# A transformer-like layer in float32 on one core: the end of the last group of steps, rewritten

## The chip, the cores and the metric

The kernel runs on one core of a Trainium2 chip. The metric is device time in microseconds of one execution, as the median of several. The engines of the core are TensorE (PE; its weight loads are listed apart as PEld), VectorE (DVE), ScalarE (ACT), GpSimd (POOL) and SyncE (SP), which only issues transfers. Each has its own queue of instructions, worked off in order, and waits on semaphores of the others.

## The reference

One layer on x (256 tokens x 2048), with a mixer block, a convolutional MLP and a last RMSNorm. Only the end of it is touched here:

```python
def conv_ffn(x, g_norm, w_up, conv_k, conv_b, w_down):
    h = rms_norm(x, g_norm)
    up = h @ w_up
    ...
    gate, val = jnp.split(up, 2, axis=-1)
    return x + (jax.nn.silu(gate) * val) @ w_down
...
    return rms_norm(x, norm_final)
```

`w_down` is 5504 x 2048. `rms_norm` divides each row by the root of its mean square (plus 1e-6) and multiplies by the weight `g`, element by element.

## The kernel before

All products of activations and weights are in a float32 form split in two: each operand is a high part (`whi`, rounded by ScalarE, L267) and a low part (`wlo`, the rest, made by VectorE, L270), and a product is three matmuls (`three_products`, L398 to L400): high by high, low by high, high by low.

The weights come in one long list of pieces of 128 x 1024 through the SP queue into five buffers `wraw`. The main loop goes through the pieces in order: for piece i it issues loads, splits the pieces up to i + 4 (`prepare`), runs the tasks that were put down for i (`at(i, f)`, `run_tasks`), and then the piece's matmuls (`steps[key](i)`). Nothing is scheduled by a tool: the order in which this loop writes the instructions is the order on each engine.

The last group of pieces is `("down", 1, 1)`: 21 row tiles of `w_down` (21 x 128 rows) for output columns 1024 to 2047. `wide_step` (L457) keeps four sums in PSUM banks, one for each (b, c): b is the block of 128 tokens (also called t), c the half of the 1024 columns; in terms of the output, column quarter q = 2 + c. Some pairs of pieces are computed with seven products instead of eight; their extra sums are put together by `combine` (L488), which is three small functions `one`, `two`, `three` of VectorE and ScalarE instructions that add into the residual `x2`.

In this last group alone the last four pieces (`LAST = 4`) are held back and done block by block: for (0,0), (0,1), (1,0) and (1,1) in turn, 4 x 3 matmuls of 512 columns finish the bank, and `done` evaluates it at once. So the last 48 matmuls are four runs of twelve.

`done` leads to `finish(p, t, q)` (L1174) for these four banks. It adds the bank to `x2` (`add_down`, L1050, or L1186), squares it on ScalarE with a running sum into `ss[:, t, q]` (L1158, L1187), and at q = 3 makes the reciprocal root of the row (`root`, L1206 to L1214), scales the row's four quarters by it (`scaled`, L1216) and issues their transfers to DRAM. The final weight `g` is multiplied in ahead of the scaling: for q = 0 and 1 on VectorE in the group before, for q = 2 on GpSimd (L1179), for q = 3 on VectorE into a tile of its own (L1192). `root` is a square root on ScalarE, a reciprocal on VectorE, and one Newton step of three VectorE instructions (L1211 to L1213).

The rows of block t = 0 go out in parts of 1024, 512 and 512 columns, those of t = 1 in parts of 896 (columns 640 to 1535, ScalarE, in its own queue), 640 and 512 (VectorE, in SP's queue).

Of the kernel before, what the change touches and what calls it, by code (L numbers as in the profile page):

```python
# [8 lines left out]
F32 = mybir.dt.float32  # L9
# [147 lines left out]
def trunk_kernel(ctx, tc, x, weights, vectors, ln_g, ln_b, w_s_turned, b_s, rpb, norm_final, out):  # L157
# [299 lines left out]
    def wide_step(key, acts, sevens, rest, done, by_block=0, fresh=None):  # L457
# [30 lines left out]
        def combine(i):  # L488
# [34 lines left out]
                at(i + 2, two_fresh)  # L523
                return
            for n, f in enumerate((one, two, three)):
                at(i + 3 if by_block else i + 1 + n, f)

        def step(i):
            n = i - n0
# [10 lines left out]
            elif n - 1 in firsts:  # L540
                k = tiles[n - 1]
                ht, lt, _ = units[i - 1, "t"]
                hs, ls, _ = units[i - 1, "s"]
                S = sevens(k)
                product(5, S[0], (ht[:, c0], lt[:, c0]))
                product(7, S[2], (ht[:, c1], lt[:, c1]))
                unit_done((i - 1, "t"))
                product(6, S[1], (hs[:, c1], ls[:, c1]))
                product(4, acts(k + 1, 1), (hs[:, c0], ls[:, c0]))
                unit_done((i - 1, "s"))  # L550
                if n - 1 == firsts[-1]:
                    combine(i)
            elif n < size - by_block:
                h, l, _ = units[i]
                for (b, c), u in OUT.items():
                    cs = slice(c * 512, (c + 1) * 512)
                    product(u, acts(tiles[n], b), (h[:, cs], l[:, cs]))
                unit_done(i)
            elif n == size - 1:
                for (b, c), u in OUT.items():  # L560
                    for m in range(size - by_block, size):
                        h, l, _ = units[n0 + m]
                        cs = slice(c * 512, (c + 1) * 512)
                        product(u, acts(tiles[m], b), (h[:, cs], l[:, cs]))
                    done(p(u), b, c, i + 1)
                    free(p(u))
                for m in range(size - by_block, size):
                    unit_done(n0 + m)
            if n == size - 1 and not by_block:
# [603 lines left out]

    def finish(p, t, q):  # L1174
        x2, ss = rs["x2"], fin["ss"]
        if q == 2:
            add_down(p, t, 2)
            v = x2[:, t, 1024:1536]
            nc.gpsimd.tensor_mul(v, v, fin["g", 2])  # L1179
            if t == 0:  # L1180
                first_squares(0)
            else:
                scaled(0, 1024, 1536, nc.vector, nc.sync)
            return
        v = x2[:, t, 1536:]
        nc.vector.tensor_add(v, p, v)  # L1186
        nc.scalar.activation(junk, v, AF.Square, accum_out=ss[:, t, 3:4])  # L1187
# [4 lines left out]
        nc.vector.tensor_mul(y, v, fin["g", 3])  # L1192
# [12 lines left out]

    def root(t):  # L1206
        a, r, q, e, both = (const.tile([128, 1], F32, name=f"{n}3{t}") for n in "arqeb")
        nc.vector.tensor_scalar(a, fin["ss"][:, t, 3:4], 1.0 / D, fin["part", t], op0=OP.mult, op1=OP.add)
# [3 lines left out]
        nc.vector.tensor_scalar(e, e, -0.5, 1.5, op0=OP.mult, op1=OP.add)  # L1212
        nc.vector.tensor_mul(both, r, e)  # L1213
        fin["r", t] = both  # L1214

    def scaled(t, c0, c1, engine, queue):  # L1216
        v, r = rs["x2"][:, t, c0:c1], fin["r", t]
        u = fin["y", t] if c1 == D else v
        if engine is nc.scalar:
            nc.scalar.activation(v, u, AF.Copy, scale=r)  # L1220
        else:
            nc.vector.tensor_scalar(v, u, r, None, op0=OP.mult)
        queue.dma_start(out[0, t * 128:(t + 1) * 128, c0:c1], v)


# [70 lines left out]

    before = {}

    def open_attention():
        xin_st.close()  # L1300
        A, at_pool["st"] = pool("attn")
        at_pool["p"] = A
# [3 lines left out]
        at_pool["v"] = A.tile([128, NBLK, NAW], F32, name="vw")  # L1306
        bias_start(starts["u", 1] + 2, 0)

    before["u", 1] = open_attention

    def open_merge():
        G_st.close()
        mg["p"], mg["st"] = pool("merge", "right")

    before["qk", 0] = open_merge

    def close_attention():
        assert at_pool["done"] == HEADS // 2
# [14 lines left out]
    before["branch", 0, 1] = close_attention  # L1333
    rs["ss"] = const.tile([128, NT, 4], F32, name="ss_2")

    def open_x2():
        mg["st"].close()
        y_st.close()
        xp, xp_st = pool("x2", "right")
# [5 lines left out]
        ctx.push(f_st)  # L1345
        more_units(p)

    at(starts["out", 0] + 2, open_x2)

    def open_ff():  # L1350
        mg["m_st"].close()
        ff["a"], fa_st = pool("act")
        ctx.push(fa_st)

        def open_conv():
            ff["p"], conv_st = pool("conv", "right")
            ctx.push(conv_st)

        at(starts["up", 0] + 3, open_conv)

    before["up", 0] = open_ff
    fin["ss"] = const.tile([128, NT, 4], F32, name="ss_3")

    def load_fin():
# [55 lines left out]
```

## Time and profile before

| | us |
|---|---|
| median of 3 runs | 1310.52 (1310.21 to 1310.73) |
| the profiled execution's own time | 1310.8 |
| its span, first to last instruction | 1308.7 |
| PE busy in the span | 1296.1 |
| DVE, ACT, POOL busy | 1015.0, 746.4, 100.6 |
| DMA, mean over the span | 200 GB/s |
| granted TensorE clock | 0.997 of full speed |

The page of the profile lists busy times, groups of instructions by line, and the chain of work that ended last, followed back from the last instruction. Times in the timeline are microseconds from the span's start. A row of the timeline has start, duration, engine, line, operation and operands; in brackets is the idle time of the engine before it and what ended that. Tile names are cut to their stem: `x` is the residual `x2`, `h` a tile that holds a quarter of the final weight or, where L1192 writes it and L1222 reads it, its product with the fourth quarter of `x2`, `a`, `q`, `r`, `e`, `b` the one-column tiles of `root`.

### The profile page before, as it was taken

The page shows a single profiled execution, that of the slowest core. Times are in us where ns is not written, and L with a number is a line of the kernel's source. Part 1 is how long each engine was busy: PE and PEld are TensorE (multiplying, and loading weights), DVE is VectorE, ACT ScalarE, POOL GpSimd, SP SyncE. Part 2 cuts the span into 40 slices and gives each one's busy share as a digit, 9 for nine tenths or more (in the row PEclk, how much of TensorE's full clock was granted, in tenths as well). Part 3 has the DMA queues.
Part 4 walks back from the last instruction along what each step waited for, and adds up shares of the span by engine and source line. Part 5 has one row for each costly group of instructions (what it writes and reads, how often), then busy time and mean ns, then how long its engine had stood idle before and what let it go on. Part 6 is the DMA issues. An engine that isn't in the chain of part 4 may idle for free.

```text
span 1308.7 us, 18617 instructions
## 1 busy us (share of the span) xinstructions
PE 1296.1 (99%) x6754; PEld 1107.3 (85%) x6754; DVE 1015.0 (78%) x1484; ACT 746.4 (57%) x1103; POOL 100.6 (8%) x192
## 2 busy tenths in 40 slices
PE   9999999999999999999999999999999999999996
PEld 8888888888888888888888888888888888888885
DVE  6576667777588978887878787898958787869986
ACT  6755567576545555556655555564536555546553
POOL 0502065430000000000000000000000000000000
PEclk9999999999999999999999999999999999999998
DMA  9956675645647566665666656456655556646743
GB/s 347 318 177 199 206 223 185 201 162 178 192 156 246 173 203 237 224 207 179 192 194 185 200 180 207 162 184 229 210 183 192 192 193 194 192 131 225 250 152 129
DMA packets 73900, 261.42 MB, mean 200 GB/s; under 512 B 9552, under 2 KB 10704, under 8 KB 73296
## 3 DMA queue, kind: packets, MB, share of 16 engines
q1 hardware_dynamic: 69840, 252.46, 59.1%
q0 software_dynamic: 3680, 7.30, 2.1%
q8 instruction: 53, 0.87, 0.3%
q10 hardware_dynamic: 288, 0.47, 0.1%
q14 instruction: 39, 0.32, 0.1%
HBM read 256.00 MB, written 2.10 MB: 197 GB/s over the span
## 4 chain that ended last, share of the span: by engine, by line
PE 96%; DVE 1%; DMA 1%; ACT 1%; issue 0%; POOL 0%; ACTq 0%; POOLq 0%; DVEq 0%
PE bank L374 31%; PE bank L382 16%; PE bank L398 15%; PE bank L400 15%; PE bank L399 15%; PE bank L415 1%; PE bank L416 1%; PE bank L418 1%; DMA wraw<-in_weights_dram 1%; PE bank L878 1%; DVE wlo L270 0%; PE bank L930 0%; PE bank L609 0%; DVE x L1044 0%; PE bank L752 0%
## 5 line engine op out<-in xcount | busy, mean ns | idle before, releaser
L270 DVE TENSOR_TENSOR wlo<-wraw,whi 128x1024 fp32r<-128x1024 f32 (+1 forms) x476 | 569.3, 1214 | 143.4 <-ACT whi L267 132.4
L267 ACT ACTIVATE whi<-wraw 128x1024 fp32r<-128x1024 f32 (+1 forms) x476 | 487.9, 1046 | 221.5 <-PE bank L399 72.7
L374 PE MATMUL bank<-h,whi 128*128 128x512 f32 x1760 | 415.8, 391 | 0.0
L374 PEld LDWEIGHTS bank<-h,whi 128*128 128x128 f32 x1760 | 324.6, 188 | 64.4
L382 PEld LDWEIGHTS bank<-h,wlo 128*128 128x128 f32 x1760 | 215.9, 188 | 6.1
L382 PE MATMUL bank<-h,wlo 128*128 128x256 f32 x1760 | 218.7, 280 | 0.0
L398 PE MATMUL bank<-whi,h 128*128 128x512 f32 x284 | 111.9, 394 | 0.0
L400 PE MATMUL bank<-wlo,h 128*128 128x512 f32 x284 | 110.7, 390 | 0.0
L399 PE MATMUL bank<-whi,h 128*128 128x512 f32 x284 | 110.6, 389 | 0.0
L744 DVE TENSOR_TENSOR ta<-bank,tb 128x256 f32<-128x256 f32 x110 | 39.0, 416 | 76.6 <-ACT tb L742 76.6
L742 ACT ACTIVATE tb<-bank 128x256 f32<-128x256 f32 x110 | 36.2, 384 | 106.5 <-PE bank L374 101.9
L400 PE MATMUL bank<-wlo,a 128*128 128x512 f32 x248 | 96.6, 389 | 0.0
L398 PE MATMUL bank<-whi,a 128*128 128x512 f32 x248 | 96.5, 389 | 0.0
L399 PE MATMUL bank<-whi,a 128*128 128x512 f32 x248 | 96.5, 389 | 0.0
L1107 ACT ACTIVATE tc<-ta,vec 128x256 f32<-128x256 f32 x86 | 47.1, 595 | 84.3 <-DVE ta L1105 84.3
L398 PEld LDWEIGHTS bank<-whi,h 128*128 128x128 f32 x284 | 53.3, 188 | 11.3 <-DVE g L518 0.4
L400 PEld LDWEIGHTS bank<-wlo,h 128*128 128x128 f32 x284 | 53.3, 188 | 11.3
L399 PEld LDWEIGHTS bank<-whi,h 128*128 128x128 f32 x284 | 53.4, 188 | 10.6
L400 PEld LDWEIGHTS bank<-wlo,a 128*128 128x128 f32 x248 | 46.5, 188 | 10.1 <-DVE wlo L270 0.4
L398 PEld LDWEIGHTS bank<-whi,a 128*128 128x128 f32 x248 | 46.6, 188 | 9.7
L399 PEld LDWEIGHTS bank<-whi,a 128*128 128x128 f32 x248 | 46.5, 188 | 9.6
L1367 POOL DMA_DIRECT2D h<-in_norm_final_dram x4 | 2.2, 540 | 669.8 <-PE bank L382 669.1
(208 smaller groups left out, 1586.3 us busy)
## 6 DMA issues: line engine op xcount, KB each, us to landing
wraw<-in_weights_dram SPq DMA_DIRECT2D x446, 512.0 KB, 4.4
start<-in_weights_dram SPq DMA_DIRECT2D x13, 640.0 KB, 6.0
xs<-in_x_dram SPq DMA_DIRECT2D x2, 1024.0 KB, 8.2
vw<-va POOLq DMA_DIRECT2D x32, 64.0 KB, 6.0
x<-in_x_dram POOLq DMA_DIRECT2D x2, 1024.0 KB, 8.5
wraw<-in_weights_dram SPq DMA_DIRECT2D x8, 256.0 KB, 2.8
run<-in_rpb_dram POOLq DMA_DIRECT2D x64, 31.2 KB, 4.1
start<-in_weights_dram SPq DMA_DIRECT2D x3, 384.0 KB, 4.9
```

What stands on the lines that cost most here:

```text
L267: nc.scalar.activation(h, w, AF.Copy)
L270: nc.vector.tensor_sub(l, w, h.bitcast(F32))
L374: nc.tensor.matmul(p, h[:, c:c + 128], acts(2 * n + k), start=n == 0 and k == 0, stop=n == last and k == tiles - 1)
L382: nc.tensor.matmul(p[:, :T], l[:, c:c + 128], acts(2 * n + k)[:, 0, :], start=False, stop=False)
L398: nc.tensor.matmul(p, xh, wh, start=start, stop=False)
L399: nc.tensor.matmul(p, xl, wh, start=False, stop=False)
L400: nc.tensor.matmul(p, xh, wl, start=False, stop=stop)
L415: nc.tensor.matmul(p, xh, h[:, cs], start=n == 0, stop=False)
L416: nc.tensor.matmul(p, xl, h[:, cs], start=False, stop=False)
L742: nc.scalar.activation(t, p[:, T:], AF.Copy)
L744: nc.vector.tensor_add(a, p[:, :T], t)
L1107: nc.scalar.activation(v, u, AF.Identity, scale=ck[:, 1, ch:ch + 1], bias=ck[:, 3, ch:ch + 1])
```

## The change

Seven things, all in the last group:

- The bank (1,1) is finished in two halves. Twelve matmuls of 256 columns finish columns 0 to 255 of the bank; then the whole bank of 512 columns is added to `x2`, where columns 256 to 511 still lack the last four pieces. Twelve more matmuls of 256 columns put these four pieces into a fresh bank, and `last_quarter` adds it.
- The sums of squares of t = 1, q = 3 are taken in two instructions of 256 columns, the second into a tile `ss_q`.
- GpSimd does no multiplication any more. At t = 0, q = 2 the weight is multiplied on VectorE. For t = 0, q = 3 and for t = 1, q = 2 and 3, weight and scale are one instruction on VectorE (`scalar_tensor_tensor`: x times r times g).
- The Newton step works on -4 times the mean square, so that its last two instructions become one.
- `root` and the scaling of the first 1024 columns of t = 0 are moved from the evaluation of (0,1) to the start of that of (1,0), before its add.
- The rows of t = 1 go out in four parts of 512 columns, two scaled by ScalarE (one in SP's queue, one in ScalarE's), two by VectorE (in SP's queue).
- The function `one` of `combine` runs a piece earlier in this group (`i + 2` instead of `i + 3`).

Some inner functions are also renamed (`open_attention` to `firstattention` and the like), which changes no instruction.

```diff
             for n, f in enumerate((one, two, three)):
-                at(i + 3 if by_block else i + 1 + n, f)
+                at(i + (2, 3, 3)[n] if by_block else i + 1 + n, f)
...
             elif n == size - 1:
+                rows = range(size - by_block, size)
+
+                def products(q, b, c0, c1, first):
+                    for m in rows:
+                        h, l, _ = units[n0 + m]
+                        three_products(q, acts(tiles[m], b), (h[:, c0:c1], l[:, c0:c1]), first and m == rows[0],
+                                       m == rows[-1])
+
                 for (b, c), u in OUT.items():
-                    for m in range(size - by_block, size):
-                        h, l, _ = units[n0 + m]
-                        cs = slice(c * 512, (c + 1) * 512)
-                        product(u, acts(tiles[m], b), (h[:, cs], l[:, cs]))
+                    if (b, c) != (1, 1):
+                        products(p(u), b, c * 512, (c + 1) * 512, False)
+                        done(p(u), b, c, i + 1)
+                        free(p(u))
+                        continue
+                    products(p(u)[:, :256], b, 512, 768, False)
                     done(p(u), b, c, i + 1)
                     free(p(u))
+                    q = bank()
+                    products(q[:, :256], b, 768, 1024, True)
+                    last_quarter(q[:, :256])
+                    free(q)
...
     def finish(p, t, q):
         x2, ss = rs["x2"], fin["ss"]
-        if q == 2:
-            add_down(p, t, 2)
-            v = x2[:, t, 1024:1536]
-            nc.gpsimd.tensor_mul(v, v, fin["g", 2])
-            if t == 0:
-                first_squares(0)
-            else:
-                scaled(0, 1024, 1536, nc.vector, nc.sync)
+        v = x2[:, t, q * 512:(q + 1) * 512]
+        if (t, q) == (1, 2):
+            root(0, ss[:, 0, 3:4])
+            scaled(0, 0, 1024, nc.scalar, nc.sync)
+        if (t, q) == (1, 3):
+            add_rest(p, t, q)
+            nc.scalar.activation(junk[:, :256], v[:, :256], AF.Square, accum_out=ss[:, 1, 3:4])
             return
-        v = x2[:, t, 1536:]
+        add_down(p, t, q)
+        if (t, q) == (0, 3):
+            nc.vector.tensor_mul(x2[:, 0, 1024:1536], x2[:, 0, 1024:1536], fin["g", 2])
+            first_squares(0)
+        if (t, q) == (1, 2):
+            scaled(0, 1024, 1536, nc.vector, nc.sync)
+            scaled(0, 1536, 2048, nc.vector, nc.sync)
+
+    def last_quarter(p):
+        v, s = rs["x2"][:, 1, 1792:], const.tile([128, 1], F32, name="ss_q")
         nc.vector.tensor_add(v, p, v)
-        nc.scalar.activation(junk, v, AF.Square, accum_out=ss[:, t, 3:4])
-        if t == 1:
-            first_squares(1)
-            scaled(0, 1536, 2048, nc.vector, nc.sync)
-        y = fin["y", t] = hpool.tile([128, 512], F32, name=f"h{t}")
-        nc.vector.tensor_mul(y, v, fin["g", 3])
-        root(t)
-        if t == 0:
-            scaled(0, 0, 1024, nc.scalar, nc.sync)
-        else:
-            scaled(1, 640, 1536, nc.scalar, nc.scalar)
-            scaled(1, 0, 640, nc.vector, nc.sync)
-            scaled(1, 1536, 2048, nc.vector, nc.sync)
+        nc.scalar.activation(junk[:, :256], v, AF.Square, accum_out=s)
+        first_squares(1)
+        part = fin["part", 1]
+        nc.vector.scalar_tensor_tensor(part, fin["ss"][:, 1, 3:4], -4.0 / D, part, op0=OP.mult, op1=OP.add)
+        root(1, s)
+        scaled(1, 0, 512, nc.scalar, nc.sync)
+        scaled(1, 1024, 1536, nc.vector, nc.sync)
+        scaled(1, 512, 1024, nc.scalar, nc.scalar)
+        scaled(1, 1536, 2048, nc.vector, nc.sync)
...
-        nc.vector.tensor_scalar(part, part, 1.0 / D, RMS_EPS, op0=OP.mult, op1=OP.add)
+        nc.vector.tensor_scalar(part, part, -4.0 / D, -4.0 * RMS_EPS, op0=OP.mult, op1=OP.add)
...
-        nc.vector.tensor_scalar(a, fin["ss"][:, t, 3:4], 1.0 / D, fin["part", t], op0=OP.mult, op1=OP.add)
-        nc.scalar.activation(q, a, AF.Sqrt)
+        nc.vector.tensor_scalar(a, s, -4.0 / D, fin["part", t], op0=OP.mult, op1=OP.add)
+        nc.scalar.activation(q, a, AF.Sqrt, scale=-1.0)
         nc.vector.reciprocal(r, q)
         nc.vector.scalar_tensor_tensor(e, r, r, a, op0=OP.mult, op1=OP.mult)
-        nc.vector.tensor_scalar(e, e, -0.5, 1.5, op0=OP.mult, op1=OP.add)
-        nc.vector.tensor_mul(both, r, e)
+        nc.vector.tensor_scalar(both, e, 3.0, r, op0=OP.add, op1=OP.mult)
...
-            nc.scalar.activation(v, u, AF.Copy, scale=r)
+            nc.scalar.activation(v, v, AF.Copy, scale=r)
+        elif c1 == 1536 and t == 0:
+            nc.vector.tensor_scalar(v, v, r, None, op0=OP.mult)
         else:
-            nc.vector.tensor_scalar(v, u, r, None, op0=OP.mult)
+            nc.vector.scalar_tensor_tensor(v, v, r, fin["g", c0 // 512], op0=OP.mult, op1=OP.mult)
```

Two places show how instructions stand on VectorE. The first is the last weight split. Before, VectorE had these rows in its queue, from the split of the last piece but one (`wlo0_12350`) on; `comb0` and `comb1` are the tiles of `combine`, `bank5` is the sum of (0,0):

```order
L270 TENSOR_TENSOR wlo0_12350<-wraw2_12282,whi0_12349 128x1024 [waits DMAHW7_49,PE_49,Activation_49]
L270 TENSOR_TENSOR wlo1_12366<-wraw3_12300,whi1_12365 128x1024 [waits DMAHW0_49,PE_49,Activation_49]
L1044 TENSOR_TENSOR x2_5087<-x2_5087,comb0_12331 128x512 [waits Activation_49]
L496 TENSOR_TENSOR comb0_12331<-comb0_12331,bank6_12170 128x512 [waits DVE_49]
L497 TENSOR_TENSOR comb1_12332<-comb0_12331,bank0_12166 128x512 [waits DVE_49]
L1044 TENSOR_TENSOR x2_5087<-x2_5087,comb0_12331 128x512
```

With the change the same place of VectorE's queue reads:

```order
L270 TENSOR_TENSOR wlo0_12350<-wraw2_12282,whi0_12349 128x1024 [waits DMAHW7_49,PE_49,Activation_49]
L1058 TENSOR_TENSOR x2_5087<-x2_5087,comb0_12331 128x512 [waits Activation_49]
L496 TENSOR_TENSOR comb0_12331<-comb0_12331,bank6_12170 128x512 [waits DVE_49]
L497 TENSOR_TENSOR comb1_12332<-comb0_12331,bank0_12166 128x512 [waits DVE_49]
L270 TENSOR_TENSOR wlo1_12370<-wraw3_12300,whi1_12369 128x1024 [waits DMAHW0_49,PE_49,Activation_49]
L1058 TENSOR_TENSOR x2_5087<-x2_5087,comb0_12331 128x512
```

The split of the last piece has moved behind the three instructions of `one`; on ScalarE the copy of L494 has likewise moved ahead of the last L267.

The second place is the end of VectorE's queue, from the add of the last bank on (`bank4` is the sum of (1,1)). Before:

```order
L1186 TENSOR_TENSOR x2_5087<-bank4_12068,x2_5087 128x512 [waits PE_49]
L1203 TENSOR_REDUCE part1_12468<-ss_3_164 128x1 [waits Activation_49]
L1204 TENSOR_SCALAR part1_12468<-part1_12468 128x1 [waits DVE_49]
L1222 TENSOR_SCALAR x2_5087<-h0_12422,b30_12428 128x512
L1192 TENSOR_TENSOR h1_12473<-x2_5087,h5_11748 128x512
L1208 TENSOR_SCALAR a31_12475<-ss_3_164,part1_12468 128x1 [waits DVE_49,Activation_49]
L1210 RECIPROCAL r31_12476<-q31_12477 128x1 [waits Activation_49]
L1211 SCALAR_TENSOR_TENSOR e31_12478<-r31_12476,a31_12475 128x1 [waits DVE_49]
L1212 TENSOR_SCALAR e31_12478<-e31_12478 128x1 [waits DVE_49]
L1213 TENSOR_TENSOR b31_12479<-r31_12476,e31_12478 128x1 [waits DVE_49]
L1222 TENSOR_SCALAR x2_5087<-x2_5087,b31_12479 128x640 [waits DVE_49]
L1222 TENSOR_SCALAR x2_5087<-h1_12473,b31_12479 128x512
```

With the change (`bank2` holds the second half of the columns):

```order
L1064 TENSOR_TENSOR x2_5087<-bank4_12068,x2_5087 128x512 [waits PE_49]
L1208 TENSOR_TENSOR x2_5087<-bank2_12466,x2_5087 128x256 [waits DVE_49,PE_49]
L1221 TENSOR_REDUCE part1_12482<-ss_3_164 128x1 [waits Activation_49]
L1222 TENSOR_SCALAR part1_12482<-part1_12482 128x1 [waits DVE_49]
L1212 SCALAR_TENSOR_TENSOR part1_12482<-ss_3_164,part1_12482 128x1 [waits DVE_49,Activation_49]
L1227 TENSOR_SCALAR a31_12486<-ss_q_12479,part1_12482 128x1 [waits DVE_49,Activation_49]
L1229 RECIPROCAL r31_12487<-q31_12488 128x1 [waits Activation_49]
L1230 SCALAR_TENSOR_TENSOR e31_12489<-r31_12487,a31_12486 128x1 [waits DVE_49]
L1231 TENSOR_SCALAR b31_12490<-e31_12489,r31_12487 128x1 [waits DVE_49]
L1241 SCALAR_TENSOR_TENSOR x2_5087<-x2_5087,b31_12490,h4_11746 128x512 [waits DVE_49]
L1241 SCALAR_TENSOR_TENSOR x2_5087<-x2_5087,b31_12490,h5_11748 128x512
```

Between the last add and the root's first instruction (L1208 before, L1227 now) the two 512-column instructions L1222 and L1192 are gone, and only one-column instructions stand there.

More of the change, by code (lines that the diff above doesn't have):

```diff
@@ L1203, in first_squares, with root @@
         nc.vector.tensor_reduce(part, fin["ss"][:, t, 0:3], axis=AX.X, op=OP.add)
-        nc.vector.tensor_scalar(part, part, 1.0 / D, RMS_EPS, op0=OP.mult, op1=OP.add)
-    def root(t):
+        nc.vector.tensor_scalar(part, part, -4.0 / D, -4.0 * RMS_EPS, op0=OP.mult, op1=OP.add)
+    def root(t, s):
         a, r, q, e, both = (const.tile([128, 1], F32, name=f"{n}3{t}") for n in "arqeb")
-        nc.vector.tensor_scalar(a, fin["ss"][:, t, 3:4], 1.0 / D, fin["part", t], op0=OP.mult, op1=OP.add)
-        nc.scalar.activation(q, a, AF.Sqrt)
+        nc.vector.tensor_scalar(a, s, -4.0 / D, fin["part", t], op0=OP.mult, op1=OP.add)
+        nc.scalar.activation(q, a, AF.Sqrt, scale=-1.0)
         nc.vector.reciprocal(r, q)
         nc.vector.scalar_tensor_tensor(e, r, r, a, op0=OP.mult, op1=OP.mult)
-        nc.vector.tensor_scalar(e, e, -0.5, 1.5, op0=OP.mult, op1=OP.add)
-        nc.vector.tensor_mul(both, r, e)
+        nc.vector.tensor_scalar(both, e, 3.0, r, op0=OP.add, op1=OP.mult)
         fin["r", t] = both
@@ L1217, in scaled @@
         v, r = rs["x2"][:, t, c0:c1], fin["r", t]
-        u = fin["y", t] if c1 == D else v
         if engine is nc.scalar:
-            nc.scalar.activation(v, u, AF.Copy, scale=r)
+            nc.scalar.activation(v, v, AF.Copy, scale=r)
+        elif c1 == 1536 and t == 0:
+            nc.vector.tensor_scalar(v, v, r, None, op0=OP.mult)
         else:
-            nc.vector.tensor_scalar(v, u, r, None, op0=OP.mult)
+            nc.vector.scalar_tensor_tensor(v, v, r, fin["g", c0 // 512], op0=OP.mult, op1=OP.mult)
         queue.dma_start(out[0, t * 128:(t + 1) * 128, c0:c1], v)
@@ L1297, in trunk_kernel, with firstattention @@
     before = {}
-    def open_attention():
+    def firstattention():
         xin_st.close()
@@ L1307, in open_attention, with firstmerge @@
         bias_start(starts["u", 1] + 2, 0)
-    before["u", 1] = open_attention
-    def open_merge():
+    before["u", 1] = firstattention
+    def firstmerge():
         G_st.close()
         mg["p"], mg["st"] = pool("merge", "right")
-    before["qk", 0] = open_merge
+    before["qk", 0] = firstmerge
     def close_attention():
@@ L1334, in trunk_kernel, with firstx2 @@
     rs["ss"] = const.tile([128, NT, 4], F32, name="ss_2")
-    def open_x2():
+    def firstx2():
         mg["st"].close()
@@ L1346, in open_x2, with firstff @@
         more_units(p)
-    at(starts["out", 0] + 2, open_x2)
-    def open_ff():
+    at(starts["out", 0] + 2, firstx2)
+    def firstff():
         mg["m_st"].close()
@@ L1353, in open_ff, with firstconv @@
         ctx.push(fa_st)
-        def open_conv():
+        def firstconv():
             ff["p"], conv_st = pool("conv", "right")
             ctx.push(conv_st)
-        at(starts["up", 0] + 3, open_conv)
-    before["up", 0] = open_ff
+        at(starts["up", 0] + 3, firstconv)
+    before["up", 0] = firstff
     fin["ss"] = const.tile([128, NT, 4], F32, name="ss_3")
```

## The prediction, made before the change was timed

> **What bounds the kernel now.** I read the page first, then the chain that ended last.
>
> ```profile
> span 1308.7 us, 18617 instructions
> ...
> PE 96%; DVE 1%; DMA 1%; ACT 1%; issue 0%; POOL 0%; ACTq 0%; POOLq 0%; DVEq 0%
> ```
>
> TensorE carries 96% of the chain. The change leaves all but the last twelve matmuls alone, so what it can win lies behind TensorE's end. I read that stretch in the timeline, instruction by instruction (start, duration, engine, line, idle time before and its releaser).
>
> ```profile
> 1294.57 0.39 PE L398 MATMUL bank<-whi,a 128*128 128x512 f32 x1
> ...
> 1297.06 0.39 PE L400 MATMUL bank<-wlo,a 128*128 128x512 f32 x1
> ...
> 1297.49 0.69 DVE L1186 TENSOR_TENSOR x<-bank,x 128x512 f32<-128x512 f32 x1
> ...
> 1298.25 1.26 POOL L1179 TENSOR_TENSOR x<-x,h 128x512 f32<-128x512 f32 x1 [3.62 <-ACT junk L1158]
> 1298.27 0.63 ACT L1187 ACTIVATE junk<-x 128x512 f32<-128x512 f32 x1
> ...
> 1298.47 1.33 DVE L1222 TENSOR_SCALAR x<-h,b 128x512 f32<-128x512 f32 x1
> ...
> 1299.72 0.68 DVE L1192 TENSOR_TENSOR h<-x,h 128x512 f32<-128x512 f32 x1
> 1300.32 0.20 DVE L1208 TENSOR_SCALAR a<-ss,part 128x1 f32<-128x1 f32 x1
> ...
> 1301.24 0.15 DVE L1212 TENSOR_SCALAR e<-e 128x1 f32<-128x1 f32 x1
> 1301.43 0.16 DVE L1213 TENSOR_TENSOR b<-r,e 128x1 f32<-128x1 f32 x1
> 1301.63 0.55 DVE L1222 TENSOR_SCALAR x<-x,b 128x640 f32<-128x640 f32 x1
> 1301.69 1.04 ACT L1220 ACTIVATE x<-x,b 128x896 f32<-128x896 f32 x1 [0.93 <-DVE b L1213]
> 1302.10 0.48 DVE L1222 TENSOR_SCALAR x<-h,b 128x512 f32<-128x512 f32 x1
> ...
> 1302.21 0.33 SPq L1223 DMA_DIRECT2D out_dram<-x  x1
> ...
> 1302.76 0.35 ACTq L1223 DMA_DIRECT2D out_dram<-x  x1
> ```
>
> The last matmul starts at 1297.06 and the last rows (block t=1) are issued to DRAM from 1302.21: 5.15 us in which VectorE and ScalarE finish the norm. Behind that lies the transfer, which I read by stretches (length, busy of PE, PEld, DVE, ACT, POOL, granted clock, DMA share, GB/s):
>
> ```profile
> 1300.75:1301.25 0.50, 0.00 (x0) 0.00 (x0) 0.39 (x3) 0.01 (x1) 0.00 (x0) 0.50 1.04 385
> 1302.75:1303.00 0.25, 0.00 (x0) 0.00 (x0) 0.00 (x0) 0.00 (x0) 0.00 (x0) 0.50 0.00 0
> ...
> 1303.00:1305.75 2.75, 0.00 (x0) 0.00 (x0) 0.00 (x0) 0.00 (x0) 0.00 (x0) 0.50 1.00 381
> ...
> 1306.00:1308.70 2.70, 0.00 (x0) 0.00 (x0) 0.00 (x0) 0.00 (x0) 0.00 (x0) 0.50 0.00 0
> ```
>
> The issue at 1302.21 has its first packets at about 1303.0, 0.8 us later. Then the 1 MB of block t=1 (381 GB/s x 2.75 us) goes out with all 16 engines full and no gap. The remaining 2.7 us, landing and closing, have no transfer in them. So from the **first** issue of block t=1 to the span's end, 6.5 us are fixed as long as the later parts arrive in time to keep the engines full. The end moves with that first issue, not with the last one.
>
> **The change, part by part.** I follow the new instructions from TensorE's end to the first issue.
>
> *Two halves.* The last twelve 512-column matmuls become 24 with 256 columns. Before, from 1294.57 to 1297.06 there are eleven steps of 0.227 us. The shape 128x256 is in the trace elsewhere, also with one weight load each:
>
> ```profile
> 1102.12 2.38 PE L382 MATMUL bank<-h,wlo 128*128 128x256 f32 x19
> ...
> L382 PEld LDWEIGHTS bank<-h,wlo 128*128 128x128 f32 x1760 | 215.9, 188 | 6.1
> L382 PE MATMUL bank<-h,wlo 128*128 128x256 f32 x1760 | 218.7, 280 | 0.0
> ...
> L744 DVE TENSOR_TENSOR ta<-bank,tb 128x256 f32<-128x256 f32 x36 | 12.8, 416 | 26.8 <-ACT tb L742 26.8
> ```
>
> With 280 ns for a single one, 18 steps take 2.10 us, 0.117 each. The 24th starts at 1294.57 + 23 x 0.117 = 1297.26. VectorE's add began 0.43 after the last start at 0.39 us a matmul; at 0.28 that is 0.32, so the new add starts at 1297.58: **0.09 lost**. As bounds: steps of 0.114 (half of 0.227) below, and above the 0.19 us that one weight load takes (188 ns), which would be +1.7 us. I take 0.117, the same form measured. The last add has 256 columns: 0.42 (L744, from PSUM) instead of 0.69. L1187 came 0.78 behind its add; now it is 0.42 + 0.10 = 0.52: **0.26 won**. The first half's 512-column add and its square must be over by then; I come to that below.
>
> *The square* of 256 columns:
>
> ```profile
> L1031 ACT ACTIVATE a<-full 128x512 fp32r<-128x512 f32 x4 | 2.5, 633 | 3.1 <-DVE full L1119 3.1
> ...
> L1031 ACT ACTIVATE a<-full 128x256 fp32r<-128x256 f32 x1 | 0.4, 418 | 0.8 <-DVE full L1119 0.8
> ```
>
> 0.633 - 0.418 = 0.21 less. How soon the root can follow a square, block t=0 shows:
>
> ```profile
> 1293.34 1.29 POOL L1179 TENSOR_TENSOR x<-x,h 128x512 f32<-128x512 f32 x1 [111.85 <-ACT junk L1158]
> ...
> 1294.21 0.97 DVE L1192 TENSOR_TENSOR h<-x,h 128x512 f32<-128x512 f32 x1
> 1294.27 0.63 ACT L1187 ACTIVATE junk<-x 128x512 f32<-128x512 f32 x1 [1.07 <-DVE x L1186]
> ...
> 1295.10 0.20 DVE L1208 TENSOR_SCALAR a<-ss,part 128x1 f32<-128x1 f32 x1
> ...
> 1296.41 1.16 ACT L1220 ACTIVATE x<-x,b 128x1024 f32<-128x1024 f32 x1 [0.87 <-DVE b L1213]
> ```
>
> There L1208 starts 0.83 after the square's start, so with 256 columns 0.62: **0.21 won**.
>
> *No GpSimd multiplications, weight and scale in one instruction.* For t=1, L1208 could have started at 1298.27 + 0.83 = 1299.10 but started at 1300.32, since VectorE was first in L1222 (1.33 us, until 1299.80; the same form at 1302.10 takes 0.48) and then in L1192. L1222 is stretched while POOL's L1179 runs, as is L1192 at t=0 (0.97 against 0.68). In the new order nothing 512 wide stands between the last add and the root: **1.22 won**, the largest term. What is late next is the square itself.
>
> In place of L1222 and L1192 comes one SCALAR_TENSOR_TENSOR, of which the trace has only a narrower form:
>
> ```profile
> L1112 DVE SCALAR_TENSOR_TENSOR tc<-ta,vec,tc 128x255 f32<-128x255 f32 x38 | 18.4, 484 | 1.4
> ```
>
> That is 0.07 over L744's 0.416, so I take 0.69 + 0.07 = 0.75 for 512 columns; bounds 0.69 (a plain multiply) and 0.97 (twice 0.484). The Trainium skill ("VectorE: DVE Perf Modes", The perf-mode tier table) has fp32 `tensor_scalar` from SBUF at twice the rate of `tensor_tensor`: the merged instruction gives up the fast form just behind the root. The trace agrees in direction (0.48 against 0.69 for 512 columns). By that rule alone the VectorE parts would come some 0.3 later; the sum stays, as a ScalarE part opens the transfer.
>
> *Block t=0 and the first half.* Its first square still has to wait for the combine (next part). Its root now has no wait on POOL's port: the plain multiply goes at 0.68 and L1208's successor follows the second square. I work it out at 1294.1 instead of 1295.10; the ScalarE scaling then starts at 1295.25 instead of 1296.41. On VectorE behind the root: add 0.68, scale 0.48, the new instruction 0.75, the 512-column add 0.69, so this add is over at 1297.45, before the last add may start (1297.58): cover 0.13. At the upper bound of 0.97 it costs 0.1. The 1 MB of block t=0 starts at about 1297.3 and is over at 1300.1, before t=1 needs the engines.
>
> *Shorter Newton step.* One instruction of 0.19 (L1212 to L1213) goes; the last one takes a second operand from a register tile, as L1208 does at 0.20 instead of 0.16: **0.15 won**. L1208 to the first scaling was 1.31 and becomes 1.16.
>
> *Four parts.* The first part issued is ScalarE's, 512 columns: 0.63 and 0.06 behind VectorE's start, against VectorE's 0.55 for 640 columns: **0.14 lost**. Then all of it: 1297.58 + 0.52 + 0.62 + 1.16 + 0.72 = 1300.60 for the first issue, against 1302.21. The later parts are ready at 1300.65 (VectorE), 1301.15 (ScalarE) and 1301.35 (VectorE), and an SP issue takes 0.33 to 0.38, so each is issued at 1301.4 at the latest. Packets of the first half MB run from 1301.4 to 1302.8; a part issued at 1301.4 has its packets ready at 1302.2. The engines stay full, and the 2048-byte rows of 512 columns went at 385 GB/s in the stretch from 1300.75. I cost this at nothing.
>
> *Combine one piece earlier.* The last weight split now stands behind three steps of the combine (first row: waits from 1280 on; us in total, times, longest):
>
> ```profile
> ACT whi L267 <- DMA wraw<-in_weights_dram: 2.2, 3, 1.1
> ...
> 1284.05 2.51 DVE L270 TENSOR_TENSOR wlo<-wraw,whi 128x1024 fp32r<-128x1024 f32 x2 [0.65 <-ACT whi L267]
> ...
> 1285.20 0.58 ACT L494 ACTIVATE comb<-bank 128x512 f32<-128x512 f32 x1
> ...
> 1286.47 0.68 DVE L1044 TENSOR_TENSOR x<-x,comb 128x512 f32<-128x512 f32 x1
> ...
> 1287.19 0.69 DVE L496 TENSOR_TENSOR comb<-comb,bank 128x512 f32<-128x512 f32 x1
> ...
> 1287.91 0.69 DVE L497 TENSOR_TENSOR comb<-comb,bank 128x512 f32<-128x512 f32 x1
> ...
> 1288.51 0.68 DVE L1044 TENSOR_TENSOR x<-x,comb 128x512 f32<-128x512 f32 x1
> ...
> 1288.68 0.19 PEld L400 LDWEIGHTS bank<-wlo,a 128*128 128x128 f32 x1
> ```
>
> Before, the second L270 is over at 1286.56 and TensorE reads its result from 1288.68 (the twelfth of the last step's 48 matmuls, 36 steps of 0.227 before the last): 2.1 us of cover. Now: the combine's first step at 1285.2, then 0.72, 0.72 and 0.60 (the spacings above), the split at 1287.24, over at 1288.46. **Cover 0.2 us.** I cost it at nothing; if a weight piece lands later, TensorE waits one for one. The rest of the combine is as much work as before, only in another order.
>
> **Sum:** -0.09 + 0.26 + 0.21 + 1.22 + 0.15 - 0.14 = 1.6 us less. From the profiled execution, 1310.8 (span 1308.7 and 2.1 around it), that makes 1309.2; the median, 1310.52, lies 0.3 under that execution, so I predict **1308.9**. A measurement of this kernel can tell about 0.2% (2.6 us) from no change: this gain counts as no change.
>
> **Rivals.**
> 1. *TensorE waits for the late split.* The cover is 0.2 us. ScalarE's splits in the last 30 us waited for their pieces to land, up to 1.1 us, and a piece 1 us later would cost 0.8: gain 0.8, **1309.7**. Against it: the last piece itself is no later than before. Chance 0.2.
> 2. *Each part pays its own start.* If the 0.8 us between issue and packets were not hidden behind the part ahead, a fourth part adds 0.8: **1309.7**. Against it: 381 GB/s without a gap over three parts. The Trainium skill ("DMA: Bandwidth & Descriptors", Rules for kernel authors) advises transfers of 1 MiB and more, which speaks against four small parts. Chance 0.07.
> 3. *The short matmuls don't overlap.* If each of the 24 paid its weight load and itself in turn, 0.19 + 0.28 = 0.47, they would take 11.3 us instead of 2.7: 8.6 more, 7.0 net, **1315.9**, slower. It turns slower from a step of (2.7 + 1.6) / 24 = 0.18 us. Against it stand 19 in a row at 0.117. Chance 0.02.
> 4. *More is won than I see:* the closing behind the last packet, of which I count nothing as won, shrinks by 1 us and more because the last transfer is 256 KB from SP instead of 448 KB from ScalarE's queue. A gain over 2.6, **1307.8**; no row gives it. Chance 0.08.
> 5. *Hidden anyway:* something else holds the 2.7 us behind the last packet, and the time stays, **1310.5**. The stretch is idle on every engine and follows the last landing. Chance 0.05.
>
> **How the numbers follow.** My forecast has the remaining 0.58 and its own range, 1308.3 to 1309.4 (0.3 us for the small terms and 0.3 for the median). With 1 and 2, 1307.9 to 1310.1 holds some 0.85. Faster by over 0.2% (under 1307.9): 0.08. Slower by over 0.2% (over 1313.1): rival 3, 0.02. Same: 0.90.
>
> **What would show it.** Right: the new L1208 (256 columns) starts some 0.3 after the last matmul's start, the root's first instruction follows the last square with VectorE idle before it, no stretched DVE instruction is left, the first issue of block t=1 comes 1.6 earlier, and the four parts run without a gap. Wrong: idle PE before the wlo matmul of the last piece; 256-column steps over 0.12; a DMA share under 0.9 between the first and last packet of t=1; or time lost outside the last 25 us.

## The result, and the profile after

The changed kernel takes **1315.76 us** (median of 5 runs, 1314.75 to 1315.96) against 1310.47 for the kernel before (5 runs, 1309.37 to 1310.73): ratio 1.004, 95% interval 1.0026 to 1.0055. It is 5.3 us slower where 1.6 us less were forecast, outside the range and on the other side.

From the page of the profile after: the span, the busy times and the chain that ended last.

```profile
span 1314.0 us, 18643 instructions
...
PE 1304.2 (99%) x6766; PEld 1108.1 (84%) x6766; DVE 1015.6 (77%) x1483; ACT 746.8 (57%) x1106; POOL 97.6 (7%) x190
...
PE 99%; DVE 0%; ACT 0%; DVEq 0%; POOL 0%; issue 0%; POOLq 0%
```

TensorE was busy for 1296.1 us before and is for 1304.2 now, although the change only puts 24 matmuls of half the width in place of twelve. (The share of TensorE in the chain, 96% before and 99% now, tells nothing of this: the kernel of experiment 1 below is 8 us faster than this one and shows 99% too.) The end, in the timeline of the kernel after:

```profile
1305.26 0.28 PE L400 MATMUL bank<-wlo,a 128*128 128x256 f32 x1
1305.58 0.42 DVE L1208 TENSOR_TENSOR x<-bank,x 128x256 f32<-128x256 f32 x1 [0.50 <-PE bank L400]
...
1306.10 0.42 ACT L1209 ACTIVATE junk<-x 128x256 f32<-128x256 f32 x1 [0.41 <-DVE part L1221]
...
1306.64 0.21 DVE L1227 TENSOR_SCALAR a<-ss_q,part 128x1 f32<-128x1 f32 x1
...
1307.82 1.33 ACT L1237 ACTIVATE x<-x,b 128x512 f32<-128x512 f32 x2 [0.73 <-DVE b L1231]
1307.82 1.41 DVE L1241 SCALAR_TENSOR_TENSOR x<-x,b,h 128x512 f32<-128x512 f32 x2
```

| us | before | after | difference |
|---|---|---|---|
| start of the last matmul | 1297.06 | 1305.26 | +8.20 |
| from there to the first issue of block t=1 | 5.15 | 3.31 | -1.84 |
| from that issue to the end of the span | 6.51 | 5.46 | -1.05 |
| span | 1308.7 | 1314.0 | +5.3 |

So the end, to which the prediction was confined, won 2.9 us, and 8.2 us were lost ahead of it, where the change does not touch the matmuls. Where, the stretches show (length, busy of PE, PEld, DVE, ACT, POOL, granted clock, DMA share, GB/s). Before:

```profile
0.00:330.00 330.00, 328.62 (x1780) 280.44 (x1781) 227.00 (x356) 212.66 (x358) 94.78 (x184) 1.00 0.69 220
330.00:512.00 182.00, 181.99 (x833) 150.49 (x832) 145.29 (x188) 94.25 (x115) 1.13 (x2) 1.00 0.59 195
512.00:1000.00 488.00, 488.00 (x2573) 420.55 (x2572) 391.50 (x558) 269.99 (x381) 0.00 (x0) 1.00 0.61 199
```

After:

```profile
0.00:330.00 330.00, 328.62 (x1780) 280.62 (x1781) 228.05 (x356) 212.49 (x358) 94.33 (x184) 1.00 0.68 219
330.00:512.00 182.00, 182.00 (x819) 148.30 (x819) 143.52 (x186) 92.99 (x112) 1.13 (x2) 1.00 0.58 191
512.00:1000.00 488.00, 488.00 (x2553) 417.11 (x2552) 391.16 (x556) 270.15 (x379) 0.00 (x0) 1.00 0.60 197
```

Up to 330 us the same 1780 matmuls fit in. Then PE is busy all the time in both, at a granted clock of 1.00, and gets through 14 and 20 matmuls less. It is not waiting; it is slower. A piece of the timeline of the branch stage (moving operand `whi` or `wlo`, 512 columns; stationary operand `y`, an activation) shows by how much, first before, then after:

```profile
341.99 0.39 PE L399 MATMUL bank<-whi,y 128*128 128x512 f32 x1
...
343.80 0.39 PE L398 MATMUL bank<-whi,y 128*128 128x512 f32 x1
```

```profile
341.04 0.40 PE L400 MATMUL bank<-wlo,y 128*128 128x512 f32 x1
...
343.84 0.39 PE L400 MATMUL bank<-wlo,y 128*128 128x512 f32 x1
```

Before, eight steps take 1.81 us, 0.226 each; after, twelve take 2.80, **0.2333** each. Not all matmuls are slower. In the groups (busy, mean ns, idle before), before and after, `y` goes from 49.8 us to 50.6, while `h` keeps its 110.6:

```profile
L399 PE MATMUL bank<-whi,h 128*128 128x512 f32 x284 | 110.6, 389 | 0.0
...
L399 PE MATMUL bank<-whi,y 128*128 128x512 f32 x128 | 49.8, 389 | 0.0
```

```profile
L399 PE MATMUL bank<-whi,h 128*128 128x512 f32 x284 | 110.6, 389 | 0.0
...
L399 PE MATMUL bank<-whi,y 128*128 128x512 f32 x128 | 50.6, 395 | 0.0
```

What differs between `y` and `h` is the place in memory. The tiles of a core are stacked from two sides of the memory of each partition; `const` (small tiles), the weights, `h`, `a` and others lie one behind the other on the left, `y`, `x2` and others on the right. The new tile `ss_q` is one column in `const`, and there it takes 32 bytes. Byte addresses in the two programs:

```
             whi0    h0      a0       y0
before       21984   87520   120288   196576
after        22016   87552   120320   196576
```

Everything behind it on the left moves by 32 bytes, nothing on the right does. From `whi0` to `y0` it was 174592 bytes, a multiple of 256; now it is 174560. The distance of `whi0` to `h0` stays. (In later stages two of the six pairs of weight buffers, `whi4` and `whi5` with their `wlo`, lie on the right too, where `y` was; there the products with these two change their distance.) That gave the **address theory**: a matmul step is slower when moving and stationary operand lie at an unlucky distance. Its rival was that the new code or its order costs the time.

### The profile page after: what moved, and what is told of

It reads as the page before. It is cut to its first block, busy times and chain, and to the rows that moved or that the text cites. A ratio compares the mean times of both kernels' runs of the same rounds, so it can differ in the third digit from the quotient of the medians.

```text
span 1314.0 us, 18643 instructions
## 1 busy us (share of the span) xinstructions
PE 1304.2 (99%) x6766; PEld 1108.1 (84%) x6766; DVE 1015.6 (77%) x1483; ACT 746.8 (57%) x1106; POOL 97.6 (7%) x190
## 4 chain that ended last, share of the span: by engine, by line
PE 99%; DVE 0%; ACT 0%; DVEq 0%; POOL 0%; issue 0%; POOLq 0%
PE bank L374 31%; PE bank L398 16%; PE bank L382 16%; PE bank L399 16%; PE bank L400 16%; PE bank L415 1%; PE bank L416 1%; PE bank L418 1%; PE bank L892 1%; PE bank L944 0%; PE bank L623 0%; PE bank L766 0%; PE bank L1008 0%; PE bank L933 0%; PE bank L1092 0%; PE bank L647 0%
## 5 line engine op out<-in xcount | busy, mean ns | idle before, releaser
L267 ACT ACTIVATE whi<-wraw 128x1024 fp32r<-128x1024 f32 (+1 forms) x476 | 487.9, 1045 | 225.1 <-PE bank L399 80.4
L399 PE MATMUL bank<-whi,h 128*128 128x512 f32 x284 | 110.6, 389 | 0.0
L399 PE MATMUL bank<-whi,a 128*128 128x512 f32 (+1 forms) x252 | 97.9, 388 | 0.0
L398 PE MATMUL bank<-whi,a 128*128 128x512 f32 (+1 forms) x252 | 97.9, 388 | 0.0
L400 PE MATMUL bank<-wlo,a 128*128 128x512 f32 (+1 forms) x252 | 97.7, 388 | 0.0
L1124 DVE SCALAR_TENSOR_TENSOR tc<-ta,vec,tc 128x255 f32<-128x255 f32 x86 | 41.4, 481 | 14.4 <-ACT tc L1121 14.4
```

Of the source, the lines that this page charges most:

```text
L267: nc.scalar.activation(h, w, AF.Copy)
L398: nc.tensor.matmul(p, xh, wh, start=start, stop=False)
L399: nc.tensor.matmul(p, xl, wh, start=False, stop=False)
L400: nc.tensor.matmul(p, xh, wl, start=False, stop=stop)
L1124: nc.vector.scalar_tensor_tensor(v[:, 1:], u[:, :T - 1], ck[:, 0, ch:ch + 1], v[:, 1:], op0=OP.mult, op1=OP.add)
```

## The experiments

All have their own runs of the kernel before beside them, 1310.1 to 1310.5 us in the median. Intervals are 95%.

**1. No new tile.** The sum goes to a column of an old tile.

```diff
-        v, s = rs["x2"][:, 1, 1792:], const.tile([128, 1], F32, name="ss_q")
+        v, s = rs["x2"][:, 1, 1792:], rs["ss"][:, 0, 0:1]
```

> The changed kernel, but the sum of the last square goes into a column of an older tile that is no longer read, instead of the new one-column tile ss_q; so every tile lies at the address that it had before the change. Address theory (the new tile takes 32 bytes a partition and shifts the weights and activations against the tiles on the other side of the memory, and 512-column matmuls on such a pair take 0.2333 us a step instead of 0.2267): the branch stage's matmuls on y are back at 0.2267 a step, the last matmul starts at about 1297.3 and not 1305.3, and the time is about 1307.8 us (my recorded sum alone would give 1308.9; the shorter closing seen after the change is worth another 1.1). Rival (the loss comes from the new code, the order of the instructions or the end of the group): the time stays at 1315.8 us, with y at 0.2333.

Measured: **1307.66 us** (ratio to before 0.9981, 0.9972 to 0.999). One operand of two instructions at the very end is another, and 8 us are gone. The stretches of this kernel:

```profile
330.00:512.00 182.00, 182.00 (x834) 150.63 (x833) 145.49 (x187) 95.05 (x117) 1.13 (x2) 1.00 0.59 194
512.00:1000.00 488.00, 488.00 (x2573) 420.81 (x2572) 391.33 (x559) 270.17 (x380) 0.00 (x0) 1.00 0.61 199
```

834 and 2573 matmuls, where the kernel before has 833 and 2573. The last matmul starts at 1296.58. This is also a version that beats both kernels.

**2. The kernel before, shifted.**

```diff
-    const.tile([128, 56], F32, name="line")
+    const.tile([128, 64], F32, name="line")
```

> The kernel before, with an unused tile of the constants 32 bytes a partition longer (64 floats instead of 56) and no other edit; the weights and activations shift as in the changed kernel. Address theory: the time rises by the 7 to 8.6 us that the changed kernel lost before TensorE's end, to 1317.5 to 1319 us, and the branch stage's matmuls on y take 0.2333 us a step. Rival (the change's own instructions cost the time): it stays at 1310.5 us and 0.2267.

Measured: 1316.98 us (1.0051, 1.0039 to 1.0064), 6.9 more. An unused tile, 32 bytes longer, does to the old kernel what the change did, a little less than expected. PE's busy time shows it too: 1303.9 us against 1296.1.

```profile
PE 1303.9 (99%) x6754; PEld 1108.3 (84%) x6754; DVE 1015.8 (77%) x1484; ACT 746.0 (57%) x1103; POOL 100.6 (8%) x192
```

With these two the cause is shown from both sides. The next four, on the changed kernel with its `ss_q`, ask which property of the address counts.

**3. Left side 32 bytes up and right side 32 down, 64 in all; 4. left side up by 64; 5. left side up by 128; 6. left 32 up and right 224 down, 256 in all.** The pad of experiment 3 (56 columns in 6); in 4 and 5 the tile `line` is longer, as in experiment 2 (64 and 80 columns):

```diff
+    keep("pad", "right").tile([128, 8], F32, name="pad")
```

> The changed kernel with its new tile, and on the other side of the memory 32 bytes of padding a partition too, so that the distance between the two sides differs by 64 bytes from that of before and no longer by 32. If the distance of moving and stationary operand counts, modulo 64 bytes: about 1307.8 us, y at 0.2267 a step. If the place of the left tiles themselves counts (they stay 32 bytes off a multiple of 64), or the distance modulo 128: 1315.8 us, y at 0.2333.

> The changed kernel with an unused tile of the constants 32 bytes longer, so that the left side lies 64 bytes further than before instead of 32. If 64 bytes are the period: about 1307.8 us, y at 0.2267 a step. If the period is 128 bytes: 1315.8 us or more, y at 0.2333.

> The changed kernel with its new tile and an unused tile of the constants 96 bytes longer, so that the left side lies 128 bytes further than before the change. Distances of 32 and 64 bytes cost 7 and 6.5 us; if the period is 128 bytes, the steps are as before the change: about 1307.7 us, y at 0.2267 a step. If the period is longer, or the cost comes from the new tile and not from the shift: 1314 us or more.

> The changed kernel with its new tile (left side 32 bytes further) and 224 bytes of padding a partition on the other side, so that the distance of the two sides differs by 256 bytes from that of before, while no tile that TensorE reads lies where it did. If the distance counts, modulo 256 bytes (32, 64, 128, 192 and 224 off were all slow): 1307.7 us, y at 0.2267 a step. If the place of each tile itself counts, or the new tile, or a longer period: 1314 us or more, y at 0.23 or more.

Measured: 1314.17, 1314.38, 1315.97 and **1307.51** us (for the last 0.9981, 0.9972 to 0.999). My first form of the theory, 64 bytes as the period, fell with the first two, and 128 with the third. Only the distance of 256 brings the time back, though there every operand of these products lies elsewhere than in the kernel before, and the new tile is in place. Its stretches again hold as many matmuls as those of the kernel before:

```profile
330.00:512.00 182.00, 182.00 (x835) 150.87 (x834) 145.57 (x188) 94.76 (x117) 1.13 (x2) 1.00 0.59 195
512.00:1000.00 488.00, 488.00 (x2573) 420.65 (x2572) 391.20 (x559) 269.90 (x380) 0.00 (x0) 1.00 0.61 199
```

So neither the place of one tile nor the new tile counts, but the distance. How many matmuls on `y` start in a fixed 30 us show these rows of the stretches, of `y` alone (length, busy of PE, PEld, DVE, ACT, granted clock, DMA share, GB/s), for the kernel before, the kernel after, experiment 3 and experiment 5:

```profile
470.00:500.00 30.00, 28.11 (x122) 22.40 (x121) 0.00 (x0) 0.00 (x0) 1.00 0.57 176
```

```profile
470.00:500.00 30.00, 28.11 (x119) 21.80 (x118) 0.00 (x0) 0.00 (x0) 1.00 0.54 173
```

```profile
470.00:500.00 30.00, 28.11 (x121) 22.22 (x120) 0.00 (x0) 0.00 (x0) 1.00 0.54 173
```

```profile
470.00:500.00 30.00, 28.11 (x120) 21.98 (x119) 0.00 (x0) 0.00 (x0) 1.00 0.55 174
```

Within the same 28.11 us 122, 119, 121 and 120 matmuls start. Over a whole kernel I took every step of the main products (from the start of one matmul to the start of the next, 0.20 to 0.25 us, so without pauses) and put it under the distance of its moving operand to the stationary operand that is loaded meanwhile, that of the next matmul, modulo 256 bytes. Means for 512 columns, followed by another matmul of 512 columns where the row does not say otherwise:

```
distance   steps   mean us   in the kernel
0          4503    0.2273    before
0          4496    0.2273    256 in all (experiment 6)
0          3222    0.2276    after
32          834    0.2333    after
224         438    0.2335    after
64          834    0.2291    left by 64
192         438    0.2333    left by 64
128        1272    0.2327    left by 128
32           68    0.2345    before, ahead of a matmul of 256 columns
64           68    0.2263    experiment 7 below, the same steps
```

In the kernel after, the 834 steps at 32 are 0.0060 us longer than those of the kernel before and the 438 at 224 are 0.0062 longer: together 7.7 of the 8.2 us. The steps at 0 of the same kernel, 0.2276, have almost the old pace, so it is not a general slowdown of that kernel. The stationary operand in use mostly lies at the same distance as the next one. Where they differ in the kernel after, 16 steps with the one in use at 32 and the next at 0 take 0.2333 us, and 18 with the next at 32 and the one in use at 0 take 0.2350: each alone goes with the longer step. With the left side up by 64 neither does (0.2271 and 0.2257). Why is open, as is why 64 costs less than 192, and no run here shows what in the memory or in TensorE makes the distance count.

**7. The low halves elsewhere.** On experiment 1, to see whether the rule also sells something: `LOW_AT` 48 in place of 56, the place of the low halves for the 256-column products.

> The changed kernel at the addresses of before, with the low halves of the 256-column products placed 32 bytes lower in their tiles (LOW_AT 48 instead of 56), so that their distance from the moving operand goes from 32 to 64 bytes modulo 256. In the shifted kernels 440 such steps at 64 bytes took 0.1156 us and 1191 at 32 bytes 0.1170. Distance theory: the 1617 steps go from 0.1168 to 0.1156, 1.9 us less, 1305.8 us. Rival (those 440 were faster for another reason, their tiles or their place): the step stays at 0.117 and the time at 1307.7; other rival: what 256-column matmuls win, the 512-column ones beside them lose, 1307.7 or more.

Measured: 1310.49 us, 2.8 more than experiment 1: a miss. In the groups (busy, mean ns, idle before) of experiment 1 and of this one

```profile
L374 PE MATMUL bank<-h,whi 128*128 128x512 f32 x1760 | 415.8, 391 | 0.0
L382 PE MATMUL bank<-h,wlo 128*128 128x256 f32 x1760 | 218.7, 280 | 0.0
```

```profile
L374 PE MATMUL bank<-h,whi 128*128 128x512 f32 x1760 | 416.7, 391 | 0.0
L382 PE MATMUL bank<-h,wlo 128*128 128x256 f32 x1760 | 220.5, 280 | 0.0
```

both rise, by 0.9 and 1.8 us. The 256-column steps at 64 bytes took 0.1177 us and not 0.1156. Why the 440 in the shifted kernels were faster at the same distance stays open; the table holds for 512 columns and for the pairs of operands in it.

**8. One GpSimd multiplication again**, on experiment 1. Now the end: of the 2.9 us won there 1.05 lay behind the first issue, which the prediction took as fixed.

```diff
         nc.vector.tensor_add(v, p, v)
+        nc.gpsimd.tensor_mul(fin["g", 0][:, :256], v, fin["g", 1][:, :256])
```

> The changed kernel at the addresses of before (first experiment), and one multiplication of 128x256 on GpSimd behind the last add, whose result nothing reads. Theory (GpSimd's closing ends some 8.4 us after its last multiplication, and before the change that held the program's end): the multiplication ends about 1 us behind the last add, so the span ends some 9 us behind it instead of 6.7; the stretch from the first issue of block t=1 to the end grows from 5.5 to 7 us or more, and the time by 1.5 to 2.3 us, to 1309.2 to 1310. Rival (the closing follows the last transfer alone): no more than the 0.7 us that a stretched VectorE instruction can cost, and an unchanged stretch from the first issue to the end.

Measured: 1309.9 us, 2.2 more than experiment 1. From the first issue to the end it takes 7.15 us (1300.44 to 1307.59) instead of 5.46. Another 0.35 us come between the last matmul and that issue, where an instruction of VectorE on one column took 0.52 us while GpSimd worked, and 0.16 in experiment 1 (first experiment 1, then this one):

```profile
1297.68 0.16 DVE L1212 SCALAR_TENSOR_TENSOR part<-ss,part 128x1 f32<-128x1 f32 x1
```

```profile
1297.66 0.72 POOL L1209 TENSOR_TENSOR h<-x,h 128x256 f32<-128x256 f32 x1 [116.86 <-DVE part L1222]
...
1297.89 0.52 DVE L1213 SCALAR_TENSOR_TENSOR part<-ss,part 128x1 f32<-128x1 f32 x1
```

The waits of SP at the closing, for experiment 1 and for this one (total, times, longest):

```profile
SPq L1434 <- PEq L1434: 0.7, 2, 0.5
```

```profile
SPq L1435 <- PEq L1435: 2.4, 2, 1.9
```

The profile names PE, but PE is long done. The raw record of GpSimd's closing instruction (a drain) has the answer; start and end in us:

```
                        last multiplication ends   its drain ends   behind it
before                  1299.51                    1307.93          8.42
experiment 2            1306.12                    1314.54          8.42
experiment 8            1298.39                    1306.81          8.42
```

In the kernel after and in experiment 1 GpSimd has no drain of over 0.1 us in the last 20 us.

**9. The kernel before without its two GpSimd multiplications.**

```diff
-            nc.gpsimd.tensor_mul(v, v, fin["g", 2])
```

> The kernel before without its two multiplications on GpSimd at the end; nothing takes their place, so columns 1024 to 1535 of the result lack their weight. All addresses stay. Closing theory (GpSimd's closing, 8.4 us behind its last multiplication, held the program's end): the stretch from the first issue of block t=1 to the end shrinks from 6.5 to 5.5 us; my recorded queue term in part: the scaling behind the last add takes 0.48 us instead of 1.33, so the root starts up to 0.7 us earlier. Together 1.7 us less than before, 1308.5 us. Rival (the closing got shorter through the four parts and the smaller last transfer): the stretch stays at 6.5 us and only the 0.7 us are won, 1309.5. If the stretched instruction held nothing either: 1310.2.

Measured: 1308.2 us (0.9984, 0.9975 to 0.9993), 2.3 less than before; nothing takes the place of the multiplications, so a quarter of the columns goes out without its weight. From the last matmul to the first issue 4.17 us (5.15 before), from there to the end 5.07 (6.51). With the three parts of before and its last transfer of 448 KB, the closing still shrinks by 1.4 us: it was GpSimd, not the form of the transfers. SP's wait, first before, then here:

```profile
SPq L1415 <- PEq L1415: 2.0, 2, 1.5
```

```profile
SPq L1414 <- PEq L1414: 0.7, 2, 0.5
```

**10. The combine's first piece where it was; 11. the last block undivided**, both on experiment 1.

```diff
-                at(i + (2, 3, 3)[n] if by_block else i + 1 + n, f)
+                at(i + 3 if by_block else i + 1 + n, f)
```

```diff
-                    products(p(u)[:, :256], b, 512, 768, False)
+                    products(p(u), b, 512, 1024, False)
...
-                    q = bank()
-                    products(q[:, :256], b, 768, 1024, True)
-                    last_quarter(q[:, :256])
-                    free(q)
...
```

In 11 the rest of the edit drops the second add, makes one square of 512 columns of the two and takes the sum from its column.

> The changed kernel at the addresses of before, with the combine's first piece put back one weight piece later, where it was before the change. My recorded step (moving it costs nothing): the time stays within 0.3 us of the first experiment's 1307.7, and TensorE waits in neither. Rival (the late split costs TensorE time in the changed kernel, cover of 0.2 us used up): this kernel is 0.4 to 0.9 us faster and shows no idle PE before the wlo matmuls of the last piece, while the first experiment does. Other rival (the move is what brings block t=0 out in time): it is slower by up to 0.7.

> The changed kernel at the addresses of before, with the last block undivided: twelve matmuls of 512 columns, one add and one square of 512. My recorded terms (0.26 + 0.21 - 0.09): the first scaling of block t=1 comes 0.4 us later behind the last weight step, the time rises by 0.4 us to 1308.1. Rival (the halves bring nothing, another instruction is late): the scaling does not move and the time stays at 1307.7.

Measured: 1307.75 us for the combine, the same as experiment 1 (1307.66). TensorE has no pause to lose: no step is over 0.3 us in the last 90 us of either kernel. The last add starts 0.58 us behind the last matmul instead of 0.31 (1297.70 to 1298.28), since VectorE is still at the add before it; in the medians, 0.1 apart, this does not show. For the undivided block 1308.36 us, 0.7 more; its timeline at the end:

```profile
1297.69 0.69 DVE L1060 TENSOR_TENSOR x<-bank,x 128x512 f32<-128x512 f32 x1 [0.86 <-PE bank L400]
...
1298.47 0.63 ACT L1192 ACTIVATE junk<-x 128x512 f32<-128x512 f32 x1 [1.50 <-DVE part L1213]
...
1300.41 1.33 ACT L1229 ACTIVATE x<-x,b 128x512 f32<-128x512 f32 x2 [0.73 <-DVE b L1223]
```

The scaling comes 3.15 us behind the last matmul (1297.26), in experiment 1 2.56 (1296.58 to 1299.14).

## Why the prediction was wrong

**The step that failed** stands in its first paragraph: "The change leaves all but the last twelve matmuls alone, so what it can win lies behind TensorE's end". The instructions are left alone, their operands are not: one tile of one column moved them by 32 bytes. That costs 7 to 8 us (experiments 1 and 2), and no term and no rival of the prediction had it. "Time lost outside the last 25 us" was named only as what would make it wrong. The trace of the kernel before held a hint of the price: 4503 of its 4571 steps of 512 columns lie at distance 0 and take 0.2273 us, and the other 68, at 32, take 0.2345. All of these stand ahead of a matmul of 256 columns, but that alone does not make them longer: in experiment 7, which moves only the low halves, the same steps are at 64 and take 0.2263. And the diff shows a new tile in a pool that lies ahead of the weights, and the kernel has an unused tile named `line` and an offset `LOW_AT` whose only work is to set addresses. That could have been a rival.

On this the Trainium skill ("SBUF — State Buffer", Who interferes with whom) says that TensorE reads moving operand and weight load through two independent ports and never waits on anyone. The rule has no word on addresses; by it alone all the distances above would run alike, and the changed kernel would take 1307.7 us. The steps of 0.2273 and 0.2333 us and the time of 1315.8 do not agree with that.

**The terms behind TensorE's end** held in the order in which they were added. From the last matmul to the first issue 3.34 us were forecast (1297.26 to 1300.60) and 3.31 measured.

- Two halves: the last add starts 0.32 us behind the last matmul, as forecast. Undoing it costs 0.59 in the timeline, less the forecast's 0.09 for the matmuls, and 0.7 in the time, where the terms gave 0.26 + 0.21 - 0.09 = 0.38.
- VectorE's queue: nothing stretched stands ahead of the root, which starts 1.38 us behind the last matmul (1305.26 to 1306.64), 3.26 before. Experiment 9, which takes only GpSimd away, wins 0.98 of the way to the first issue.
- Newton step: from the root's first instruction to the scaling 1.18 us instead of 1.31, 0.12 won against 0.15.
- The new instruction of weight and scale takes 0.75 us for 512 columns (1303.74 in the timeline), the value taken.
- Block t=0: the forecast's 0.13 of cover ahead of the last add does not follow from its own terms, since 0.68, 0.48, 0.75 and 0.69 from 1295.25 on end at 1297.85 and not at 1297.45. The cover held all the same: in the trace the four start 0.60, 0.40 and 0.66 apart, they overlap, the root of t=0 comes 0.5 us earlier than forecast against the last matmul, and the last of the four is over at 1305.08, 0.50 before the last add.
- Four parts: no gap. In the stretches of the kernel after, the engines are full between the first and the last packets:

```profile
1309.50:1311.50 2.00, 0.00 (x0) 0.00 (x0) 0.00 (x0) 0.00 (x0) 0.00 (x0) 0.81 1.03 374
```

  So rival 2, a start for each part, did not come. To leave the Trainium skill's advice behind it ("DMA: Bandwidth & Descriptors", Rules for kernel authors), transfers of 1 MiB and more, cost nothing here: these parts of 256 KB overlap.
- The combine a piece earlier costs and wins nothing that the time shows; rival 1, a wait for the late split, did not come (experiment 10).

**Mis-sized:** "6.5 us are fixed" behind the first issue. They were 5.46, because 1 us and more of the closing was a wait for GpSimd and not the landing of the transfer. The row for it was there before, SP's last wait at the closing with 1.5 us; the prediction makes no use of SP's waits. Rival 4 had the right sign, "the closing behind the last packet ... shrinks by 1 us and more", and the wrong mechanism: not the smaller last transfer (experiment 9). With it the end wins 2.9 us in the trace and 2.4 in the time (1310.1 to 1307.66, experiment 1), in place of 1.6.

## What to carry to other kernels

A new tile, however small, is an edit to every address behind it in its pool's side: compare the addresses of the operands of the busiest engine before and after, and put small tiles where they move nothing, or pad so that the distance stays a multiple of 256 bytes, the only one that ran fast in these runs. When a change at one end costs time in another place, count instructions in fixed stretches with the engine fully busy: fewer of the same instructions at the same clock points to slower instructions, not to waits. And when an engine's last work lies just ahead of the program's end, look at the waits of the closing as well as at the last transfer.

## What was not expected of the hardware

- A 512-column matmul step (with its weight load beside it) took 0.2273 us when moving and next stationary operand lay a multiple of 256 bytes apart, and 0.2291 to 0.2335 at 32, 64, 128, 192 or 224 bytes more: up to 2.7% on an engine that is busy all the time, at a granted clock of 1.00.
- GpSimd's closing ended 8.42 us behind its last multiplication in three kernels (before, experiments 2 and 8), and the program ended no sooner: with a multiplication just behind the last add it, and not the last transfer, set the end (1.7 us more from the first issue on in experiment 8, 1.4 less without it in experiment 9).
- An instruction of VectorE on one column took 0.52 us instead of 0.16 while GpSimd multiplied (experiment 8), so a small instruction too was stretched.
